# Output projection of a gated attention block: seven quarter-block products in place of eight, with float32 sums as operands

## The chip, the cores and the metric

The kernel runs on one core of one Trainium2 chip, as one launch. The metric is the device time of that launch in microseconds (us). One execution was also recorded by the hardware profiler; its times are read below. The engines are called TensorE (PE; its weight loads are PEld), VectorE (DVE), ScalarE (ACT), GpSimd (POOL) and SyncE (SP, which issues most of the transfers). Each engine works through its own list of instructions strictly in order.

## The reference

One decoder layer: a combined input projection, three attention mixers A, B and C, a gated merge, an output projection, then a SwiGLU feed-forward layer. Shapes: 512 tokens, model width 1024, hidden width 2816, all float32.

```python
h = _rms(x, norm1_g)
... = _split_last(h @ w_in, IN_SIZES)           # queries, keys, values, gates mix_g
y_a, y_b, y_c = mixer_a(...) @ w_branch_a, mixer_b(...) @ w_branch_b, mixer_c(...) @ w_branch_c
g = jax.nn.sigmoid(mix_g).reshape(bsz, seq, 3, D_MODEL)
z = g[:, :, 0] * y_a + g[:, :, 1] * y_b + g[:, :, 2] * y_c
x = x + z @ w_out                               # (512 x 1024) @ (1024 x 1024): the part that is changed
h = _rms(x, norm2_g)
gate, up = jnp.split(h @ w_ffn_in, 2, axis=-1)
x = x + (jax.nn.silu(gate) * up) @ w_ffn_out
```

## The kernel before

**Products.** Every float32 product is made of three matmuls: each operand is split into a high part (rounded by ACT) and a low part (the rest, by a DVE subtraction), and high*high, high*low and low*high are added up in PSUM (`mm3`, lines 106 to 108). The helper `split` (lines 80 to 82) makes one such pair: a cast on ACT, line 81, and a subtraction on DVE or POOL, line 82, with both inputs in SBUF. `weights` loads a slice of a weight matrix into the tile `raw` (5 buffers) and splits it into `whi` and `wlo` (6 buffers each, 128x512 elements).

**The gated merge.** For the branches in the order B, A, C and eight column blocks f of 128 each, `gate(bi, f)` makes a product of 24 matmuls into a PSUM tile `pm` (3 buffers) and takes a tanh of it on ACT into `tz`; `merge(bi, f, tz)` makes the branch product (6 matmuls for C), combines it with the gate on DVE (line 973), and adds the sum of the branches so far, which comes back from DRAM (`dz`), on POOL (line 976; on DVE for the last two blocks). For branch C the result, z transposed, stays in SBUF: `zh` is its high part (ACT, line 980) and `zl` its low part (DVE, line 981). `tz` has 3 buffers.

**The output projection** (lines 1052 to 1080). The weight is taken in four slices of 256 columns; each is loaded and split by `weights`. For each slice and each of the four token tiles t there are 8 x 3 matmuls of 256 columns, in the first slice with the last two k-blocks of all tiles held back; then DVE adds the result to the residual `x2` (line 1072), ACT takes the sum of squares, and POOL (in the last slice DVE) multiplies by the norm's gain into `xg` (line 1075). In the last slice `norm_T` is started for each token tile: a reduction, the reciprocal root on POOL, a scaled copy `hn` (half on DVE, line 176, half on ACT), 8 transposes on PE, and the split into `xh2` and `xl2`. The feed-forward layer begins with the first two token tiles as soon as these are there.

The order of the instructions on each engine is set when the program is built: a scheduler replays the program with estimated costs and lists each engine's instructions; code inside `tc.high_priority()` is taken first. Pools are stacked in SBUF; a tile in a reused place waits for the last users of that place.

Of the kernel before, what the change touches and what calls it, by code (L numbers as in the profile page):

```python
# [67 lines left out]
def block_kernel(ctx: ExitStack, tc: tile.TileContext, x, norm1_g, norm2_g, w_in, qk_norm_g, cmp_pos, cmp_w,  # L68
# [153 lines left out]
    ap_ = att.enter_context(tc.tile_pool(name="att", bufs=1, reuse_waits="tile"))  # L222
    abx = ExitStack()
# [5 lines left out]
    def bias_vectors():  # L229
# [4 lines left out]
        for c in range(0, VEC, n):  # L234
            oh = ap_.tile([NB + 1, 512], F32, name="oh", tag="p", bufs=5)
# [3 lines left out]
            vs = ap_.tile([28, 512], F32, name="vs", tag="p", bufs=5)  # L239
# [47 lines left out]
    def norm_heads(tm, c0, nh):  # L287
# [3 lines left out]
        for t in range(0, NT, 2):  # L291
            sq = ap_.tile([128, 2, 256], F32, name="sq", tag="sq", bufs=1)
# [101 lines left out]
    def scores(i):  # L394
# [34 lines left out]
    def compress_inputs():  # L429
# [10 lines left out]
        def then():  # L440
            nc.gpsimd.memset(vcp, 0.0)
            for sel in range(2):
# [18 lines left out]
                if sel == 0:  # L461
                    sq = ap_.tile([64, 64], F32, name="sqc", tag="p", bufs=5)
# [59 lines left out]
    def pt_tile(n):  # L522
        return ap_.tile([128, n, 128], F32, name="pT", tag="pT", bufs=4)
# [26 lines left out]
    def causal_probs(q, i, k, tab, topk, gate):  # L550
# [8 lines left out]
        p = ap_.tile([128, S], F32, name="p", tag="p", bufs=5)  # L559
# [41 lines left out]
    def cmp_scores(g):  # L601

        def a():
# [4 lines left out]
            sT = ap_.tile([128, S], F32, name="cmpT", tag="p", bufs=5)  # L608
# [219 lines left out]
    def c_unit(hf, i, j, ld, d):  # L828
# [6 lines left out]
        def a():  # L835
# [11 lines left out]
            p = ap_.tile([128, S], F32, name="pc_", tag="p", bufs=5)  # L847
# [111 lines left out]
    def merge(bi, f, tz):  # L959
# [48 lines left out]
    def ready(bi):  # L1008
# [21 lines left out]
    zh, zl = zs["h"], zs["l"]  # L1030
# [134 lines left out]
```

## Time and profile before

| what | value |
|---|---|
| device time, median of 3 runs | 995.63 us (993.09 to 1602.01) |
| the profiled execution, device time | 995.54 us |
| its span, from the first to the last instruction | 993.8 us |
| PE busy, share of the span | 974.3 us, 98% |
| DVE, ACT, POOL busy | 568.1, 437.5, 175.4 us |
| mean granted TensorE clock | 0.993 of full speed |

The profiled execution lies 0.09 us below the median, so times read from its trace stand for the median as they are; 1.7 us of the device time lie outside the span. The highest of the three runs stands alone and is not used. Busy shares are averages over stages with different limits; the stage of the change is 48 us long.

### The profile page before, as it was taken

The page shows a single profiled execution, that of the slowest core. Times are in us where ns is not written, and L with a number is a line of the kernel's source. Part 1 is how long each engine was busy: PE and PEld are TensorE (multiplying, and loading weights), DVE is VectorE, ACT ScalarE, POOL GpSimd, SP SyncE. Part 2 cuts the span into 40 slices and gives each one's busy share as a digit, 9 for nine tenths or more (in the row PEclk, how much of TensorE's full clock was granted, in tenths as well). Part 3 has the DMA queues.
Part 4 walks back from the last instruction along what each step waited for, and adds up shares of the span by engine and source line. Part 5 has one row for each costly group of instructions (what it writes and reads, how often), then busy time and mean ns, then how long its engine had stood idle before and what let it go on. Part 6 is the DMA issues. An engine that isn't in the chain of part 4 may idle for free.

```text
span 993.8 us, 16076 instructions
## 1 busy us (share of the span) xinstructions
PE 974.3 (98%) x5887; PEld 827.0 (83%) x5887; DVE 568.1 (57%) x1277; ACT 437.5 (44%) x956; POOL 175.4 (18%) x156
## 2 busy tenths in 40 slices
PE   6999999999999999989999999999999999999998
PEld 6889999899887578858777899988888888888886
DVE  6699999766665655665764654544344444422321
ACT  5544555755665555554543434433233233322220
POOL 4135555543100202231110312000000000000000
PEclk9999999999999899989999999999999999999999
DMA  8541344433232334346613462233333323332421
GB/s 210 122 128 44 85 119 132 123 109 122 90 104 67 85 117 138 107 141 193 180 62 97 140 210 86 85 94 108 96 85 105 107 85 91 110 97 96 138 75 42
DMA packets 119264, 109.91 MB, mean 111 GB/s; under 512 B 19931, under 2 KB 105234, under 8 KB 119186
## 3 DMA queue, kind: packets, MB, share of 16 engines
q1 hardware_dynamic: 116994, 107.85, 37.4%
q10 hardware_dynamic: 2192, 1.05, 0.4%
q8 instruction: 46, 0.75, 0.3%
q14 instruction: 32, 0.26, 0.1%
HBM read 96.66 MB, written 12.21 MB: 110 GB/s over the span
## 4 chain that ended last, share of the span: by engine, by line
PE 96%; DMA 1%; DVE 1%; ACT 1%; issue 0%; SPq 0%; DVEq 0%; ACTq 0%
PE pf L108 14%; PE pf L107 14%; PE pf L106 14%; PE pm L107 13%; PE pm L106 13%; PE pm L108 13%; PE tr L111 5%; PE ovb L541 2%; PE lg L363 2%; PE lg L364 2%; PE ova L541 1%; PE lg L843 1%; DMA raw<-in_w_in 1%; PE ovc L888 1%; PE lg L838 0%
## 5 line engine op out<-in xcount | busy, mean ns | idle before, releaser
L82 DVE TENSOR_TENSOR wlo<-raw,whi 128x512 fp32r<-128x512 f32 (+1 forms) x243 | 182.5, 756 | 147.7 <-ACT whi L81 146.6
L81 ACT CAST whi<-raw 128x512 fp32r<-128x512 f32 (+1 forms) x288 | 176.8, 619 | 173.9 <-PE pf L108 78.6
L107 PE MATMUL pm<-wlo,xh 128*128 128x256 f32 (+1 forms) x512 | 145.9, 288 | 0.3 <-DVE wlo L82 0.3
L108 PE MATMUL pm<-whi,xl 128*128 128x256 f32 (+1 forms) x512 | 145.3, 286 | 0.5 <-POOL xl L82 0.5
L106 PE MATMUL pm<-whi,xh 128*128 128x256 f32 (+1 forms) x512 | 145.7, 289 | 0.0
L107 PE MATMUL pf<-xl,whi 128*128 128x512 f32 (+1 forms) x384 | 142.6, 372 | 0.1
L106 PE MATMUL pf<-xh,whi 128*128 128x512 f32 (+1 forms) x384 | 142.5, 372 | 0.0
L108 PE MATMUL pf<-xh,wlo 128*128 128x512 f32 (+1 forms) x384 | 142.0, 371 | 0.0
L107 PEld LDWEIGHTS pm<-wlo,xh 128*128 128x128 f32 x512 | 98.5, 193 | 1.9 <-issue 0.8
L108 PEld LDWEIGHTS pm<-whi,xl 128*128 128x128 f32 x512 | 98.7, 193 | 1.4 <-POOL xl L82 0.8
L106 PEld LDWEIGHTS pm<-whi,xh 128*128 128x128 f32 x512 | 98.3, 194 | 0.4
L107 PE MATMUL pm<-xl,whi 128*128 128x512 f32 x224 | 88.8, 396 | 0.0
L108 PE MATMUL pm<-xh,wlo 128*128 128x512 f32 x224 | 88.6, 395 | 0.0
L106 PE MATMUL pm<-xh,whi 128*128 128x512 f32 x224 | 88.4, 395 | 0.0
L107 PEld LDWEIGHTS pf<-xl,whi 128*128 128x128 f32 x384 | 72.3, 188 | 12.8 <-DVE xl L82 0.3
L108 PEld LDWEIGHTS pf<-xh,wlo 128*128 128x128 f32 x384 | 72.2, 188 | 12.6
L106 PEld LDWEIGHTS pf<-xh,whi 128*128 128x128 f32 x384 | 72.2, 188 | 12.3
L82 POOL TENSOR_TENSOR wlo<-raw,whi 128x512 fp32r<-128x512 f32 x45 | 62.2, 1402 | 111.6 <-ACT whi L81 100.8
L106 PE MATMUL pf<-whi,hh 128*128 128x512 f32 x176 | 69.4, 395 | 0.0
L108 PE MATMUL pf<-whi,hl 128*128 128x512 f32 x176 | 69.4, 395 | 0.0
L107 PE MATMUL pf<-wlo,hh 128*128 128x512 f32 x176 | 69.4, 395 | 0.0
L562 ACT ACTIVATE p<-p,m 128x128 f32<-128x128 f32 (+3 forms) x96 | 53.9, 562 | 28.6 <-DVE m L547 26.4
(312 smaller groups left out, 1702.3 us busy)
## 6 DMA issues: line engine op xcount, KB each, us to landing
raw<-in_w_in SPq DMA_DIRECT2D x92, 256.0 KB, 3.0
raw<-in_w_ffn_in SPq DMA_DIRECT2D x88, 256.0 KB, 2.9
raw<-in_w_ffn_out SPq DMA_DIRECT2D x44, 256.0 KB, 2.8
raw<-in_w_in SPq DMA_DIRECT2D x52, 128.0 KB, 2.4
x<-in_x SPq DMA_DIRECT2D x8, 512.0 KB, 5.9
tab<-dvec SPq DMA_DIRECT2D x16, 256.0 KB, 3.3
dz<-tz SPq DMA_DIRECT2D x16, 256.0 KB, 2.4
tz<-dz SPq DMA_DIRECT2D x16, 256.0 KB, 3.3
```

Source lines behind the costliest of these rows:

```text
L81: nc.scalar.copy(dst_hi, src)
L82: (eng or nc.vector).tensor_tensor(out=dst_lo, in0=src, in1=dst_hi.bitcast(F32), op=ALU.subtract)
L106: nc.tensor.matmul(ps, ah, bh, start=(j == 0), stop=False)
L107: nc.tensor.matmul(ps, ah, bl, start=False, stop=False)
L108: nc.tensor.matmul(ps, al, bh, start=False, stop=(j == n - 1))
L111: nc.tensor.transpose(dst, src, ident[0:src.shape[0], 0:src.shape[0]])
L363: nc.tensor.matmul(lg, qs, k[:, 0, 0:w], start=True, stop=False)
L364: nc.tensor.matmul(lg, qs, k[:, 1, 0:w], start=False, stop=stop)
L541: mm = nc.tensor.matmul(ov[64 * j:64 * j + 64, 128 * b:S], v(b), pts[j][:, 4 * b:3 * b + NT, :], start=first and b == 0, stop=last and b = ...
L562: nc.scalar.activation(p[:, 0:w], p[:, 0:w], AF.Exp, bias=m[:, 0:1], scale=-1.0, accum_out=m[:, 1:2])
L843: nc.tensor.matmul(lg[32 * r:32 * r + 32, c:c + n], ld["q", g][hp, 128 * i + 32 * r:128 * i + 32 * r + 32], ld["k", g][hp, 128 * r:128 * r ...
L888: nc.tensor.matmul(ov[h, 128 * b_:128 * q1], ld["v", 0][:, b_, h], d["pt", jj][:, 2 * b_:b_ + q1, :], start=b_ == 0, stop=False)
```

## The change

The projection z @ w_out is cut into quarter blocks: z by token halves and by even and odd blocks f (A11: second half of the tokens, even blocks; A12: the same, odd; A22: first half, odd), w_out into B11, B12, B21, B22 (k-halves by columns 0 to 511 and 512 to 1023). With sums of quarter blocks as further operands (S1 to S4 of z, T1 to T4 of w_out) seven products of 256 x 512 x 512 take the place of eight. Each product is 2 token tiles x 4 k-blocks x 3 matmuls, now of 512 columns.

What is moved and added: the weight is loaded whole by `wo_load`, in four transfers of 1 MB during branch C, into a pool of its own; that place is freed by closing a part of the attention pool early (`att2`, which is the former `att` without two tags). T3 and T2 are made on POOL at once, T1 and T4 on POOL later (`wo_operands`). `z_parts` replaces the split of each z block: per pair of blocks four sums on DVE of 128x256 and the splits of A11, of the odd block, of S2 and S4, and of S1 and S3. The seven weight operands are each split by ACT and DVE (28 splits for 16). Partial results are collected in `zu` and added to `x2` on POOL (`pool_add`), or added straight from PSUM on DVE (`add_half`).

```diff
@@ pools and places (the same edit for the tags p, sq and pT) @@
+    att2 = ExitStack()
+    a2 = att2.enter_context(tc.tile_pool(name="att2", bufs=1, reuse_waits="tile"))
...
-        p = ap_.tile([128, S], F32, name="p", tag="p", bufs=5)
+        p = a2.tile([128, S], F32, name="p", tag="p", bufs=5)
...
@@ merge, branch C @@
-            nc.scalar.mul(zs["h"][:, f, :], th, 0.5)
-            nc.vector.scalar_tensor_tensor(out=zs["l"][:, f, :], in0=th, scalar=0.5, in1=zs["h"][:, f, :].bitcast(F32),
-                                           op0=ALU.mult, op1=ALU.subtract)
+            z_parts(f // 2, f % 2, th)
+
+    T1, T2 = slice(S // 2, S), slice(0, S // 2)
+    WO_AT = (0, 2, 3, 5)
+
+    def wo_load(m):
+        raw = zs["raw"][m]
+        nc.sync.dma_start(raw, w_out[m * 256:(m + 1) * 256, :].rearrange("(k p) (n c) -> p k n c", p=128, n=2))
+        b11, b12, b22, t2 = raw[:, 0, 0, :], raw[:, 0, 1, :], raw[:, 1, 1, :], zs["t2"][m]
+        nc.gpsimd.tensor_tensor(out=b12, in0=b22, in1=b12, op=ALU.subtract)
+        nc.gpsimd.tensor_tensor(out=t2, in0=b12, in1=b11, op=ALU.add)
+
+    def z_parts(m, odd, th):
+        if not odd:
+            zs["even"] = th
+            split(zs["a11"][:, 0, m, :], zs["a11"][:, 1, m, :], th[:, T1])
+            return
+        e = zs["even"]
+        sums = []
+        for _ in range(2):
+            sums.append(zs["p"].tile([128, 2, S // 2], F32, name="zsum", tag="zsum", bufs=2))
+        (s2, s4), (s1, s3) = ([t_[:, j, :] for j in range(2)] for t_ in sums)
+        nc.vector.tensor_tensor(out=s1, in0=e[:, T2], in1=th[:, T2], op=ALU.add)
+        nc.vector.tensor_tensor(out=s2, in0=s1, in1=e[:, T1], op=ALU.subtract)
+        nc.vector.tensor_tensor(out=s4, in0=th[:, T1], in1=s2, op=ALU.subtract)
+        split(zs["s24"][:, 0, m], zs["s24"][:, 1, m], sums[0])
+        split(zs["o"][:, 0, m, :], zs["o"][:, 1, m, :], th)
+        nc.vector.tensor_tensor(out=s3, in0=e[:, T1], in1=e[:, T2], op=ALU.subtract)
+        split(zs["s13"][:, 0, m], zs["s13"][:, 1, m], sums[1])
...
+                if due[0][0] == 2 and due[0][1] in WO_AT:
+                    wo_load(WO_AT.index(due[0][1]))
                 merge(*due.pop(0))
...
@@ output projection @@
-    for c in range(0, D, 256):
-        wk = weights(w_out, [(c, 256)], list(range(KC)))
...
-            mm3(pss[t][:, 0:256], [((zh[:, k, ts], zl[:, k, ts]), wk[k]) for k in range(k0, k1)], k0, KC)
...
-            nc.vector.tensor_tensor(out=xs, in0=xs, in1=pss[t][:, 0:256], op=ALU.add)
...
+                if name == "t1":
+                    nc.gpsimd.tensor_tensor(out=b11, in0=b22, in1=t2, op=ALU.subtract)
+                elif name == "t4":
+                    nc.gpsimd.tensor_tensor(out=t2, in0=b21, in1=t2, op=ALU.subtract)
+                hi = wp.tile([128, 512], F32R, name="whi", tag="whi")
+                lo = wp.tile([128, 512], F32R, name="wlo", tag="wlo")
+                split(hi, lo, src)
...
+    def add_half(t, cs, ps):
+        nc.vector.scalar_tensor_tensor(out=x2[t][:, cs], in0=ps, scalar=0.5, in1=x2[t][:, cs], op0=ALU.mult, op1=ALU.add)
...
+    def pool_add(t, cs, u):
+        nc.gpsimd.tensor_tensor(out=x2[t][:, cs], in0=x2[t][:, cs], in1=u, op=ALU.add)
+
+    for a, b in (("a11", "b11"), ("s2", "t2"), ("a12", "b21"), ("s3", "t3"), ("s1", "t1"), ("a22", "t4"), ("s4", "b22")):
+        ws = wo_operands(b)
+        for r in range(2):
+            ps, t1, t2 = m2_tile(), NT // 2 + r, r
+            if b == "b22" and r == 1:
+                product(a, ws, ps, r, range(2))
+                next(norms[1], None)
+                product(a, ws, ps, r, range(2, HK))
+            else:
+                product(a, ws, ps, r)
+            if b == "b11":
+                us[r] = zs["p"].tile([128, 512], F32, name="zu", tag="zsum", bufs=2)
+                nc.scalar.mul(us[r], ps, 0.5)
+                pool_add(t1, C1, us[r])
+            elif b in ("t2", "t3"):
+                nc.vector.scalar_tensor_tensor(out=us[r], in0=ps, scalar=0.5, in1=us[r], op0=ALU.mult, op1=ALU.add)
+                for t, cs in ((t1, C2),) if b == "t2" else ((t2, C2), (t2, C1)):
+                    pool_add(t, cs, us[r])
+            elif b == "b21":
+                add_half(t1, C1, ps)
+                done(t1, C1, nc.gpsimd)
+            elif b == "t1":
+                add_half(t2, C2, ps)
+                add_half(t1, C2, ps)
+                done(t2, C2, nc.gpsimd)
+            elif b == "t4":
+                add_half(t2, C1, ps)
+                done(t2, C1, nc.vector)
+                norm2(t2)
+            else:
+                add_half(t1, C2, ps)
+                done(t1, C2, nc.vector)
+                norm2(t1)
+                if r == 0:
+                    next(norms[0], None)
```

Up to the merges of branch C the lists of all engines are the same as before, instruction by instruction. On POOL, from the first z block of branch C on, the list before held only the six sums with `dz` and then the multiplications by the gain:

```order
L976 TENSOR_TENSOR tz_6543<-tz_6543 128x512
L976 TENSOR_TENSOR tz_6587<-tz_6587 128x512
L976 TENSOR_TENSOR tz_6662<-tz_6662 128x512
L976 TENSOR_TENSOR tz_6701<-tz_6701 128x512
L976 TENSOR_TENSOR tz_6770<-tz_6770 128x512
L976 TENSOR_TENSOR tz_6809<-tz_6809 128x512
L1075 TENSOR_TENSOR xg0_6975<-x2_0_6960,gb2_6973 128x256
```

In the changed kernel eight sums of the weight (`wraw`, `wt2`) stand between the sums of the z blocks (`tz`); the first rows are:

```order
L993 TENSOR_TENSOR wraw0_6601<-wraw0_6601 128x512
L994 TENSOR_TENSOR wt2_0_6605<-wraw0_6601 128x512
L978 TENSOR_TENSOR tz_6546<-tz_6546 128x512
L993 TENSOR_TENSOR wraw1_6602<-wraw1_6602 128x512
L978 TENSOR_TENSOR tz_6590<-tz_6590 128x512
L994 TENSOR_TENSOR wt2_1_6606<-wraw1_6602 128x512
L978 TENSOR_TENSOR tz_6679<-tz_6679 128x512
L993 TENSOR_TENSOR wraw2_6603<-wraw2_6603 128x512
L993 TENSOR_TENSOR wraw3_6604<-wraw3_6604 128x512
L994 TENSOR_TENSOR wt2_2_6607<-wraw2_6603 128x512
L994 TENSOR_TENSOR wt2_3_6608<-wraw3_6604 128x512
L978 TENSOR_TENSOR tz_6728<-tz_6728 128x512
```

The first weight pair now stands ahead of the first z block, and weight sums ahead of most later ones; eight more (lines 1102 and 1104) and eight additions to `x2` (line 1139) follow behind.

On DVE, around the last two merges of branch C, the list before had two gate products, two sums and the two low parts of z, and then went on to the weight splits of the projection:

```order
L973 SCALAR_TENSOR_TENSOR tz_6878<-tz_6878,pm_6926 128x512
L976 TENSOR_TENSOR tz_6878<-tz_6878 128x512
L973 SCALAR_TENSOR_TENSOR tz_6917<-tz_6917,pm_6938 128x512
L82 TENSOR_TENSOR wlo_7132<-raw_7129,whi_7131 128x512
L976 TENSOR_TENSOR tz_6917<-tz_6917 128x512
L981 SCALAR_TENSOR_TENSOR zl_6594<-tz_6878,zh_6593 128x512
L981 SCALAR_TENSOR_TENSOR zl_6594<-tz_6917,zh_6593 128x512
L82 TENSOR_TENSOR wlo_7138<-raw_7135,whi_7137 128x512
```

In the changed kernel the same two merges (line 975) bring three low parts of z sums (`za11`, `zo`, `zs13`, and `zs24` of the pair before) and four sums `zsum`:

```order
L975 SCALAR_TENSOR_TENSOR tz_6921<-tz_6921,pm_6982 128x512
L82 TENSOR_TENSOR zs24_6599<-zsum_6936,zs24_6599 128x512
L978 TENSOR_TENSOR tz_6921<-tz_6921 128x512
L975 SCALAR_TENSOR_TENSOR tz_6973<-tz_6973,pm_6994 128x512
L82 TENSOR_TENSOR wlo_7102<-wt2_1_6606,whi_7101 128x512
L1011 TENSOR_TENSOR zsum_7004<-tz_6921 128x256
L82 TENSOR_TENSOR za11_6597<-tz_6921,za11_6597 128x256
L978 TENSOR_TENSOR tz_6973<-tz_6973 128x512
L1006 TENSOR_TENSOR zsum_7004<-tz_6921,tz_6973 128x256
L1007 TENSOR_TENSOR zsum_7003<-zsum_7004,tz_6921 128x256
L82 TENSOR_TENSOR zo_6598<-tz_6973,zo_6598 128x512
L1008 TENSOR_TENSOR zsum_7003<-tz_6973,zsum_7003 128x256
```

The weight splits `wlo` of the second product, which PE needs next, now stand between and behind these rows.

## Rows read from the trace of the kernel before

**Rows 1.** The page: span, engine totals, PE in 40 slices, chain by engine, ACT's casts.

```profile
span 993.8 us, 16076 instructions
...
PE 974.3 (98%) x5887; PEld 827.0 (83%) x5887; DVE 568.1 (57%) x1277; ACT 437.5 (44%) x956; POOL 175.4 (18%) x156
...
PE   6999999999999999989999999999999999999998
...
PE 96%; DMA 1%; DVE 1%; ACT 1%; issue 0%; SPq 0%; DVEq 0%; ACTq 0%
...
L81 ACT CAST whi<-raw 128x512 fp32r<-128x512 f32 (+1 forms) x288 | 176.8, 619 | 173.9 <-PE pf L108 78.6
```

**Rows 2.** Busy time by stage: branch C's merges, projection, feed-forward; columns as headed.

```profile
core 0: us, PE busy (x) PEld busy (x) DVE busy (x) ACT busy (x) POOL busy (x), PEclk, DMA share, GB/s
540.00:576.40 36.40, 36.40 (x162) 30.10 (x161) 23.73 (x30) 16.21 (x27) 9.20 (x6) 1.00 0.46 138
576.40:624.40 48.00, 48.00 (x402) 47.93 (x401) 23.89 (x46) 21.05 (x54) 12.68 (x18) 1.00 0.41 132
645.00:840.00 195.00, 195.00 (x884) 162.39 (x884) 84.39 (x126) 64.94 (x108) 0.00 (x0) 1.00 0.35 98
```

**Rows 3.** Timeline of PE: starts of 512-column matmuls, then 256-column ones.

```profile
548.08 0.39 PE L106 MATMUL pm<-xh,whi 128*128 128x512 f32 x1
...
551.25 0.39 PE L108 MATMUL pm<-xh,wlo 128*128 128x512 f32 x1
...
614.81 0.28 PE L106 MATMUL pf<-whi,zh 128*128 128x256 f32 x1
...
619.61 0.28 PE L107 MATMUL pf<-wlo,zh 128*128 128x256 f32 x1
```

**Rows 4.** Durations by tile (ns min/median/max): DVE's subtraction, POOL's sum.

```profile
L82 DVE TENSOR_TENSOR wlo<-raw,whi x122: 684/693/697, 649.3 to 974.0; 128x512 fp32r<-128x512 f32 x122
...
L976 POOL TENSOR_TENSOR tz<-tz x7: 1288/1622/1745, 520.2 to 569.5; 128x512 f32<-128x512 f32 x7
```

**Rows 5.** Timeline, POOL and DVE, 546 to 551 and 625 to 627.

```profile
546.60 2.99 POOL L976 TENSOR_TENSOR tz<-tz 128x512 f32<-128x512 f32 x2 [24.79 <-DVE tz L973]
...
545.77 1.28 DVE L973 SCALAR_TENSOR_TENSOR tz<-tz,pm 128x512 f32<-128x512 f32 x2 [0.47 <-PE pm L108]
546.98 3.16 DVE L82 TENSOR_TENSOR wlo<-raw,whi 128x512 fp32r<-128x512 f32 x2
...
625.65 0.41 DVE L1072 TENSOR_TENSOR x<-x,pf 128x256 f32<-128x256 f32 x1
625.98 1.29 DVE L82 TENSOR_TENSOR wlo<-raw,whi 128x512 fp32r<-128x512 f32 x2
```

**Rows 6.** Timeline of DVE and PE: the last norm steps, first feed-forward matmuls.

```profile
616.95 0.49 DVE L176 TENSOR_SCALAR hn<-xg,rst 128x512 f32<-128x512 f32 x1 [0.96 <-POOL rst L151]
...
619.73 1.03 PE L111 MATMUL pf<-ident,hn 128*128 128x128 f32 x8
...
624.35 0.28 PE L108 MATMUL pf<-whi,zl 128*128 128x256 f32 x1
624.47 0.28 PE L106 MATMUL pf<-xh,whi 128*128 128x256 f32 x1
```

**Rows 7.** PE's longest wait inside the kernel, and the granted clock around it.

```profile
435.54 0.87 PE L111 MATMUL tr<-ident,p 128*128 128x128 f32 x3 [3.49 <-DVE p L564]
...
426.00:433.50 7.50, 5.98 (x35) 4.14 (x29) 6.16 (x12) 3.98 (x12) 4.74 (x5) 1.00 0.33 92
433.50:440.50 7.00, 4.23 (x18) 3.25 (x18) 4.70 (x11) 3.54 (x8) 1.68 (x2) 0.51 0.30 89
```

**Rows 8.** Transfers: last attention matmuls on PE, and what a busy stretch moved.

```profile
537.42 1.96 PE L893 MATMUL ovc<-pt,c_v 128*64 128x128 f32 x29
...
577.00:584.00 7.00, 7.00 (x61) 7.00 (x60) 3.09 (x5) 1.40 (x3) 0.00 (x0) 1.00 0.72 232
```

More of the change, by code (lines that the diff above doesn't have):

```diff
@@ L522, in pt_tile @@
     def pt_tile(n):
-        return ap_.tile([128, n, 128], F32, name="pT", tag="pT", bufs=4)
+        return a2.tile([128, n, 128], F32, name="pT", tag="pT", bufs=4)
     def transposed(pt, p, i):
@@ L846, in a @@
             w = w0 + 2 * n
-            p = ap_.tile([128, S], F32, name="pc_", tag="p", bufs=5)
+            p = a2.tile([128, S], F32, name="pc_", tag="p", bufs=5)
             m = ty.tile([128, 4], F32, name="mcc", tag="m")
@@ L1015, in ready @@
         czx.close()
+        att2.close()
         zp = zx.enter_context(tc.tile_pool(name="zs", bufs=1, side="right", reuse_waits="tile"))
-        zs["h"] = zp.tile([128, KC, S], F32R, name="zh")
-        zs["l"] = zp.tile([128, KC, S], F32R, name="zl")
+        zs["p"] = zp
+        zs["a11"] = zp.tile([128, 2, KC // 2, S // 2], F32R, name="za11")
+        zs["o"] = zp.tile([128, 2, KC // 2, S], F32R, name="zo")
+        zs["s24"] = zp.tile([128, 2, KC // 2, 2, S // 2], F32R, name="zs24")
+        zs["s13"] = zp.tile([128, 2, KC // 2, 2, S // 2], F32R, name="zs13")
+        zs["raw"] = [zp.tile([128, 2, 2, 512], F32, name=f"wraw{m}") for m in range(KC // 2)]
+        zs["t2"] = [zp.tile([128, 512], F32, name=f"wt2_{m}") for m in range(KC // 2)]
     due = []
@@ new lines, in block_kernel, with wo_operands @@
+    norms = {}
+    HK = KC // 2
+    def wo_operands(name):
+        res = []
+        with tc.high_priority():
+            for m in range(HK):
+                raw, t2 = zs["raw"][m], zs["t2"][m]
+                b11, t3, b21, b22 = (raw[:, k, n, :] for k in range(2) for n in range(2))
+                src = {"b11": b11, "b21": b21, "b22": b22, "t1": b11, "t2": t2, "t3": t3, "t4": t2}[name]
+                if name == "t1":
[5 more added lines that the diff above has]
+                split(hi, lo, src)
+                res.append((hi, lo))
+        return res
@@ new lines, in block_kernel, with product @@
+    z_rows = {"a11": lambda p, m: zs["a11"][:, p, m, :], "a12": lambda p, m: zs["o"][:, p, m, T1],
+              "a22": lambda p, m: zs["o"][:, p, m, T2], "s2": lambda p, m: zs["s24"][:, p, m, 0, :],
+              "s4": lambda p, m: zs["s24"][:, p, m, 1, :], "s1": lambda p, m: zs["s13"][:, p, m, 0, :],
+              "s3": lambda p, m: zs["s13"][:, p, m, 1, :]}
+    us = [None, None]
+    C1, C2 = slice(0, 512), slice(512, D)
+    def product(a, ws, ps, r, ms=range(HK)):
+        rs = slice(128 * r, 128 * r + 128)
+        for m in ms:
+            (ah, al), (bh, bl) = (z_rows[a](p, m)[:, rs] for p in range(2)), ws[m]
+            nc.tensor.matmul(ps, ah, bh, start=m == 0, stop=False)
+            nc.tensor.matmul(ps, ah, bl, start=False, stop=False)
+            nc.tensor.matmul(ps, al, bh, start=False, stop=m == HK - 1)
@@ new lines, in add_half, with done, norm2 @@
+    def add_half(t, cs, ps):
+        nc.vector.scalar_tensor_tensor(out=x2[t][:, cs], in0=ps, scalar=0.5, in1=x2[t][:, cs], op0=ALU.mult, op1=ALU.add)
+    def done(t, cs, eng):
+        norm_sums(ss2[t], x2[t], np_, cs.start, cs.stop, 1)
+        eng.tensor_tensor(out=xg[t][:, cs], in0=x2[t][:, cs], in1=gb2[:, cs], op=ALU.mult)
+    def norm2(t):
+        norms[t] = norm_T(xg[t], t, ss2[t], 2, None, xh2, xl2, lambda: m2_tile().rearrange("p (k c) -> p k c", c=128), np_,
+                          (nc.vector, nc.vector))
+        next(norms[t])
```

40 lines of the change are left out of this document (8 added, 32 removed).

## The prediction

> **What bounds the kernel now.** I read the page first: PE is busy for 974.3 of 993.8 us and makes up 96% of the chain that ended last [rows 1]. The reader is to see that only PE's path counts, as long as nobody makes PE wait. Then the stages [rows 2]: in the merges of branch C and in the projection PE works without a gap (36.4 of 36.4 and 48.0 of 48.0 us), DVE fills 23.7 us of the first and 23.9 of the second, POOL 9.2 and 12.7; in the feed-forward layer PE has no gap either. So the change is worth what it takes from PE between 546 and 625 us, unless DVE or POOL, which get much more to do there, fall behind. The third view is therefore the timeline of DVE and POOL where both work at once [rows 5].
>
> **The matmuls.** From 548.08 to 551.25 PE starts 14 matmuls of 512 columns after the first, 0.2264 us each; from 614.81 to 619.61 it starts 40 of 256 columns, 0.120 us each [rows 3]. Before: 4 slices x 4 token tiles x 8 blocks x 3 = 384 x 0.120 = 46.1 us. After: 7 products x 2 x 4 x 3 = 168 x 0.2264 = 38.0 us. PE saves **8.1 us**; the transposes stay.
>
> **What DVE and POOL cost each other.** Alone, a DVE subtraction of 128x512 with both inputs in SBUF takes 0.69 us (0.60 from start to start: two take 1.29), a POOL sum 1.29 [rows 4, 5]. At 546.60 POOL starts two sums, and DVE behind it two subtractions; DVE ends at 546.98 + 3.16 = 550.14, so two of each took 3.54 us, 1.77 for a pair. That is the sum of the two (1.29 + 0.48), not the longer one: they take turns. The two DVE operations just before, with one input in PSUM, took 1.28 us together, as ever, though POOL had started within them [rows 5]: these don't take turns. The Trainium skill says the same in "SBUF — State Buffer", section "Who interferes with whom": a DVE instruction with two SBUF inputs and a GpSimd instruction that reads SBUF exclude each other for their whole length. By that rule the new POOL sums are no free help to DVE, and this trace agrees (1.77 us a pair).
>
> So I add up, as one queue, all that must pass that turnstile from POOL's first z sum at 546.60 to the norm's `hn` of the first token tiles, which starts at 616.95 before [rows 6].
> - POOL: 6 z sums, 6 weight sums of `wo_load` (the first two come ahead of 546.60), 8 sums for T1 and T4, 8 additions to `x2`, 4 multiplications by the gain: 32 x 1.29 = 41.3 us.
> - DVE, 128x512, both inputs in SBUF: 7 splits left of the gates and branch C, 28 of w_out, 2 of the feed-forward weight, 12 low parts of z, 2 sums with `dz`, 3 gains: 54, at 0.48 to 0.60 (rows as above). I take 0.55, between the two: 29.7 us (25.9 to 32.4).
> - DVE, 128x256: 4 low parts of A11 and 16 sums, at 0.33 (the start-to-start time of the 256-column row at 625.65 [rows 5]): 6.6 us.
>
> Together 77.6 us (73.8 to 80.3). DVE also runs 19 operations with an input in PSUM, 0.60 each, 11.4 us. They cost nothing where POOL uses the turnstile meanwhile. From the lists: for 9 of them POOL's next operation needs their result, during 2 POOL waits for a later split, and for the last 3 POOL has nothing left; 14 x 0.60 = 8.4 us are exposed (0 to 11.4). `hn` then starts at 546.6 + 77.6 + 8.4 = 632.6 (620.4 to 638.3), 15.6 us later than before.
>
> **From there to the feed-forward layer.** Before, its first matmul starts at 624.47, 7.5 us after `hn`, because PE still has two token tiles to multiply. After, PE has only the second half of the seventh product left: `hn` 0.5, 8 transposes 1.0, 12 matmuls 2.7, 8 transposes 1.0, a cast 0.6, together 5.8 us [rows 1, 3, 6]. So it starts at 638.4, **13.9 us later** (1.7 to 19.6). The rest is PE's alone, as before. This is not added to the 8.1 us: they are saved on an engine that now waits.
>
> **Who waits.** In the merges: POOL's sum of a z block stands behind weight sums, DVE's sums behind it, and `tz` has three buffers, so a tanh waits for the sums of the block three before, `pm` is freed late and PE's next merge waits. In the projection: PE's tenth matmul needs A11 of block 6, which is behind two merges' work on DVE; later PE waits for single `wlo` tiles, and before the last half product for `hn`. All this is inside the sum.
>
> **The clock.** After PE's one long wait (3.49 us) the granted clock is 0.51 of full speed, 1.2 in place of 2.4 GHz, from 433.5 to 440.5 us [rows 7]. Such a stretch costs up to 3.5 us where PE is the bound. The waits above are as long, three of them. Two fall where DVE and POOL set the pace and PE has time to spare; the last stands ahead of the feed-forward layer, where it counts. I take +2.3 us (0 to 7, two stretches).
>
> **Hidden.** ACT gets 12 more weight casts, about 6 more z casts and 2 copies, 20 x 0.62 = 12 us, and has 84.4 - 37.3 = 47 us free [rows 1, 2]. SP: the four 1 MB transfers can't start before the last attention matmuls leave their place, about 539.4; at the 232 GB/s of a busy stretch [rows 8] the first lands near 544 and the fourth near 557.5, about when POOL's queue comes to it. The gate weights queued behind them on SP come later, too; I take 0 (0 to +3).
>
> **Sum.** 995.5 (profiled, 0.1 below the median) + 13.9 + 2.3 = **1011.7 us**; its own range goes from 995.5 + 1.7 = 997 to 995.5 + 19.6 + 7 = 1022. A difference of 2% (19.9 us) is about what a measurement of this kernel can tell from no change; this one is 1.6%.
>
> **Rivals.**
> - *PE's saving stands* (not slower): DVE and POOL keep ahead, as they would if their turns overlapped: DVE's and POOL's own times are then no bound, and PE's 8.1 us come off: 987.4. For it: DVE was half idle in both stages. Against: the pair of 1.77 us; and even the smallest sum, 73.8 us with nothing exposed, ends `hn` after 616.95.
> - *The clock decides* (slower by over 2%): each long wait of PE starts a stretch at half clock, in which PE becomes the bound, too, and the DVE operations that wait for PSUM results come later. It decides from the third stretch that counts: 995.5 + 13.9 + 3 x 3.5 = 1019.9. For it: the wait of 3.49 us before such a stretch [rows 7] is no longer than these; against: PE would have spare time in two of the three.
> - *The weight comes late*: SP's queue or the transfers hold POOL's first weight sum, and with it every z block, by up to 3 us: 1014.7. The list puts that sum ahead of the first z block, so there is no way around it.
>
> **How the numbers follow.** Forecast 0.63; saving stands 0.09; clock 0.21; weight late 0.07. The predicted time is 1011.7. For 8 in 10 I leave out most of the saving (below) and the clock's upper end: 995 to 1025. Over 2% faster (below 975.7) is reached by no case; I leave 0.01. Slower by over 2% (above 1015.5): the clock rival and a part of the forecast's upper end, 0.28. Within 2%: 0.71.
>
> **What would show it.** In the changed profile: DVE's `wlo` and z operations between 546 and 632 at well over 1 us in the mean where 0.69 is their time alone, DVE and POOL almost without common idle time, PE busy for about two thirds of the projection; PE waiting in its first product for the cast of `za11`, and for `hn` before its last half product; the first feed-forward matmul near 638; matmuls of 512 columns still 0.226 us apart where nothing waits; a granted clock below 1.00 after the waits. Wrong it would be if the weight and z operations of DVE stay near 0.7 us while POOL is busy, or if PE's list runs through without waits: then the saving stands. If the merges of branch C end at 576.7 as before, the waits in them were not there.

## The result, and the profile of the changed kernel

The changed kernel takes 1007.69 us (median; 1005.00 to 1010.67) against 994.98 us for the kernel before: a ratio of 1.0135, 95% interval 1.0096 to 1.0174. That median of the kernel before counts a run of 1602.01 us that stands alone; its other three runs have a median of 994.33, and the ratio is against them. The prediction was 1011.7 us with a range of 995 to 1025. So seven products in place of eight made the kernel about 13 us slower. The profiled execution took 1007.67 us, its span is 1005.9, 12.1 more than before.

The page of the changed kernel, first the span, the engines' totals, TensorE (PE) in 40 slices, and the chain that ended last by engine:

```profile
span 1005.9 us, 15679 instructions
...
PE 971.7 (97%) x5671; PEld 813.6 (81%) x5671; DVE 609.0 (61%) x1311; ACT 445.5 (44%) x962; POOL 209.8 (21%) x172
...
PE   6999999999999999989999978999999999999998
...
PE 87%; DVE 5%; DMA 3%; issue 2%; SPq 1%; ACT 1%; POOL 1%; DVEq 0%; POOLq 0%; ACTq 0%
```

PE is busy 2.6 us less than before [rows 1], but the span grew, and the chain runs only for 87% over PE where it was 96%. The slices show where: the two that cover 578 to 629 us, in the projection, have 7 and 8 where they had 9.

Busy time by stage, in the first two windows of [rows 2] and then in four pieces of the projection:

```profile
core 0: us, PE busy (x) PEld busy (x) DVE busy (x) ACT busy (x) POOL busy (x), PEclk, DMA share, GB/s
540.00:576.40 36.40, 34.87 (x156) 28.41 (x154) 31.42 (x38) 15.42 (x28) 21.09 (x15) 1.00 0.51 161
576.40:624.40 48.00, 42.34 (x171) 33.14 (x169) 47.93 (x56) 23.36 (x45) 32.34 (x20) 0.93 0.16 60
580.00:592.20 12.20, 6.60 (x20) 4.93 (x19) 12.13 (x17) 3.69 (x7) 6.18 (x4) 0.72 0.63 236
592.20:624.00 31.80, 31.77 (x137) 25.26 (x135) 31.80 (x36) 17.43 (x34) 23.73 (x14) 1.00 0.00 1
624.00:636.00 12.00, 7.05 (x31) 5.60 (x29) 9.72 (x20) 8.06 (x17) 2.32 (x6) 0.72 0.24 66
```

In the projection the engines have changed places. VectorE (DVE) is busy for 47.93 of 48.00 us where it was 23.89, and PE, which had no gap, has 5.7 us of them. The granted clock is 1.00 except in the two short windows where PE waited.

What PE waited for between 540 and 640 us (total, times, longest):

```profile
PE pf L1122 <- ACT za L81: 5.6, 1, 5.6
PE pf L111 <- DVE hn L176: 4.6, 1, 4.6
PE pm L106 <- ACT tz L958: 1.5, 1, 1.5
PE pf L107 <- DVE nss L170: 0.6, 1, 0.6
PE pf L106 <- ACT xh L81: 0.3, 1, 0.3
```

These are 12.6 us, and the three long ones are at places that the prediction named: the merges, the tenth matmul of the first product, and the transposes of `hn` before the last half product. The timeline of PE around the wait for `hn` and the first feed-forward matmul (start, length, engine, line, operation):

```profile
623.99 0.39 PE L1124 MATMUL pf<-whi,zs 128*128 128x512 f32 x1
629.00 1.97 PE L111 MATMUL pf<-ident,hn 128*128 128x128 f32 x8 [4.63 <-DVE hn L176]
630.62 0.77 PE L1122 MATMUL pf<-whi,zs 128*128 128x512 f32 x1
631.20 0.63 PE L1123 MATMUL pf<-wlo,zs 128*128 128x512 f32 x1
631.62 0.63 PE L1124 MATMUL pf<-whi,zs 128*128 128x512 f32 x1
632.05 0.63 PE L1122 MATMUL pf<-whi,zs 128*128 128x512 f32 x1
632.48 0.63 PE L1123 MATMUL pf<-wlo,zs 128*128 128x512 f32 x1
632.90 0.47 PE L1124 MATMUL pf<-whi,zs 128*128 128x512 f32 x1
633.21 0.39 PE L1122 MATMUL pf<-whi,zs 128*128 128x512 f32 x1
633.45 0.39 PE L1123 MATMUL pf<-wlo,zs 128*128 128x512 f32 x1
...
634.38 0.40 PE L1124 MATMUL pf<-whi,zs 128*128 128x512 f32 x1
634.62 1.04 PE L111 MATMUL pf<-ident,hn 128*128 128x128 f32 x8
635.97 0.39 PE L106 MATMUL pf<-xh,whi 128*128 128x256 f32 x1 [0.32 <-ACT xh L81]
```

Three things stand in these rows. The first feed-forward matmul starts at 635.97; before it was 624.47 [rows 6]. After the wait the matmuls of 512 columns come 0.43 us apart (631.20 to 632.48: 3 in 1.28 us), the pace of the lower clock level. And at the full clock they come 0.234 us apart (633.21 to 634.38: 5 in 1.17 us), not the 0.2264 us that the gate's matmuls of the same width have [rows 3].

The timelines of VectorE and then GpSimd (POOL) in the middle of the projection:

```profile
594.03 1.78 DVE L82 TENSOR_TENSOR wlo<-wt,whi 128x512 fp32r<-128x512 f32 x1
595.74 6.40 DVE L82 TENSOR_TENSOR wlo<-wraw,whi 128x512 fp32r<-128x512 f32 x5
602.06 0.68 DVE L1156 SCALAR_TENSOR_TENSOR zu<-pf,zu 128x512 f32<-128x512 f32 x1
```

```profile
593.66 1.61 POOL L1104 TENSOR_TENSOR wt<-wraw,wt 128x512 f32<-128x512 f32 x1 [4.09 <-DVE wlo L82]
595.96 1.62 POOL L1104 TENSOR_TENSOR wt<-wraw,wt 128x512 f32<-128x512 f32 x1 [0.69 <-DVE wlo L82]
597.54 3.44 POOL L1139 TENSOR_TENSOR x<-x,zu 128x512 f32<-128x512 f32 x2
```

Five subtractions took 6.40 us beside three of POOL's operations. Alone, five take 4 x 0.60 + 0.69 = 3.1 us [rows 4, 5], so POOL's three cost VectorE 3.3 us. The single subtraction before them shows the turn itself: it starts at 594.03, 0.37 us into a sum of POOL's that ends at 595.27, and ends at 595.81, 0.54 us behind that sum.

**Where the 12.1 us came from.** The last attention matmuls end at 538.46 + 1.96 = 540.42, 1.04 us later than before [rows 8]: that difference is ahead of the change. In the merges 1.8 us are lost, 1.5 of them the wait for `tz`. The projection, from its first matmul (576.65 before, 579.53 now) to the first of the feed-forward layer, takes 56.44 us in place of 47.82, that is +8.6: its matmuls take 168 x 0.2333 = 39.2 us in place of 46.1 (-6.9), three waits add 5.60 + 4.63 + 0.32 = 10.55, and half clock adds 4.1 (from 587.38, 11 matmuls in 4.81 us where 2.57 would do; from 629.00, 8 transposes and 6 matmuls in 4.21 us, which take 2.34 in a run below that fills this wait); 0.9 is left over. Another 0.6 is the wait for `nss` behind it.

### The profile page after: what moved, and what is told of

Read it like the earlier page. It is cut to its first block, busy times and chain, and to the rows that moved or that the text cites. A ratio compares the mean times of both kernels' runs of the same rounds, so it can differ in the third digit from the quotient of the medians.

```text
span 1005.9 us, 15679 instructions
## 1 busy us (share of the span) xinstructions
PE 971.7 (97%) x5671; PEld 813.6 (81%) x5671; DVE 609.0 (61%) x1311; ACT 445.5 (44%) x962; POOL 209.8 (21%) x172
## 4 chain that ended last, share of the span: by engine, by line
PE 87%; DVE 5%; DMA 3%; issue 2%; SPq 1%; ACT 1%; POOL 1%; DVEq 0%; POOLq 0%; ACTq 0%
PE pf L107 12%; PE pf L108 12%; PE pf L106 12%; PE pm L107 11%; PE pm L106 11%; PE pm L108 11%; PE tr L111 5%; PE ovb L543 2%; PE lg L365 2%; PE lg L366 2%; DVE wlo L82 2%; PE pf L1122 1%; PE ova L543 1%; PE pf L1123 1%; PE pf L1124 1%
## 5 line engine op out<-in xcount | busy, mean ns | idle before, releaser
L82 DVE TENSOR_TENSOR wlo<-raw,whi 128x512 fp32r<-128x512 f32 (+1 forms) x227 | 170.9, 757 | 138.6 <-ACT whi L81 138.1
L81 ACT CAST whi<-raw 128x512 fp32r<-128x512 f32 (+1 forms) x272 | 166.9, 619 | 164.0 <-PE pf L108 76.1
```

The lines of the kernel that those rows point to most:

```text
L81: nc.scalar.copy(dst_hi, src)
L82: (eng or nc.vector).tensor_tensor(out=dst_lo, in0=src, in1=dst_hi.bitcast(F32), op=ALU.subtract)
```

## The experiments

My theory was the turnstile of the prediction: an operation of VectorE with two inputs in SBUF and one of POOL take turns, and the queue that they form sets `hn`. The rivals: VectorE's own work is too much, whoever makes the sums; the clock; something in the seven products themselves (their order, their pace, the transfers). Eleven kernels were run. The times are medians beside runs of the kernel before on the same chip; ratios are against the kernel before. On those chips the kernel before had medians of 994.99 to 996.05 us. The last attention matmul, ahead of the merges of branch C, ends between 537.5 and 540.8 us in the profiled executions, so the table counts `hn` from there.

| kernel | median us | ratio, 95% interval | `hn` behind the last attention matmul, us |
|---|---|---|---|
| before | 994.98 | 1 | 77.6 |
| changed | 1007.69 | 1.0135 (1.0096 to 1.0174) | 88.0 |
| e1, weight sums on VectorE | 1000.2 | 1.0047 (1.0031 to 1.0062) | 83.2 |
| e2, all those sums on VectorE | 1000.67 | 1.0049 (1.0032 to 1.0067) | 82.2 |
| e3, no operand sums | 994.43 | 0.9987 (0.9971 to 1.0004) | 76.6 |
| e5, before with 512 columns | 997.13 | 1.0024 (1.0002 to 1.0046) | 79.7 |
| e7, e2 in another order | 997.74 | 1.0028 (1.0014 to 1.0043) | 80.5 |
| e8, e1 in another order | 997.75 | 1.0020 (1.0005 to 1.0034) | 77.4 |
| e9, e3 in another order | 990.28 | 0.9938 (0.9921 to 0.9955) | 71.3 |
| e10, before with more POOL sums | 997.53 | 1.0015 (1.0000 to 1.0030) | 79.9 |
| e11, changed with waits filled | 1004.62 | 1.0096 (1.0082 to 1.0110) | 88.9 |
| e12, e7 with the wait filled | 997.78 | 1.0022 (1.0007 to 1.0036) | 79.9 |
| e13, changed in another order | 1004.09 | 1.0088 (1.0075 to 1.0101) | 83.4 |

### e1 and e2: the sums on VectorE

e1 moves the 16 weight sums:

```
-        nc.gpsimd.tensor_tensor(out=b12, in0=b22, in1=b12, op=ALU.subtract)
-        nc.gpsimd.tensor_tensor(out=t2, in0=b12, in1=b11, op=ALU.add)
+        nc.vector.tensor_tensor(out=b12, in0=b22, in1=b12, op=ALU.subtract)
+        nc.vector.tensor_tensor(out=t2, in0=b12, in1=b11, op=ALU.add)
...
-                    nc.gpsimd.tensor_tensor(out=b11, in0=b22, in1=t2, op=ALU.subtract)
+                    nc.vector.tensor_tensor(out=b11, in0=b22, in1=t2, op=ALU.subtract)
...
-                    nc.gpsimd.tensor_tensor(out=t2, in0=b21, in1=t2, op=ALU.subtract)
+                    nc.vector.tensor_tensor(out=t2, in0=b21, in1=t2, op=ALU.subtract)
```

> The changed kernel with its 16 weight sums issued on VectorE in place of GpSimd (14 of them behind the first z sum); nothing else moves. Theory of the turns (an operation of VectorE with two SBUF inputs and one of GpSimd exclude each other): each sum that leaves GpSimd takes 1.29 us out of the queue and brings back 0.55 us on VectorE, so hn starts 14 x 0.74 = 10.4 us sooner than its 628.5, near 618, and the time falls from 1007.7 to about 997 (995 to 1000). Rival of volume (VectorE is simply the fuller engine, GpSimd's sums ran beside it for nothing): 14 x 0.55 to 0.69 = 7.7 to 9.7 us more in VectorE's queue, hn near 637, the time 1015 to 1017. Rival of the clock (the half-clock stretches set the loss): they stay, and so does the time, 1005 to 1011.

e2 moves the eight additions of `pool_add` and four gains as well:

```
-        nc.gpsimd.tensor_tensor(out=x2[t][:, cs], in0=x2[t][:, cs], in1=u, op=ALU.add)
+        nc.vector.tensor_tensor(out=x2[t][:, cs], in0=x2[t][:, cs], in1=u, op=ALU.add)
...
-                done(t1, C1, nc.gpsimd)
+                done(t1, C1, nc.vector)
...
-                done(t2, C2, nc.gpsimd)
+                done(t2, C2, nc.vector)
```

> As the run with the weight sums moved, and the eight additions of the shared partial sum and the four gain products moved to VectorE as well (26 operations behind the first z sum in all; six z sums and the small rstd operations stay on GpSimd). Turns: 26 x 0.74 = 19.2 us out of the queue, hn near 609.3; the time would be 988.5, down to where TensorE's own work ends it (994.98 - 8.1 = 986.9). Volume: 26 x 0.55 to 0.69 = 14.3 to 17.9 us more, 1022 to 1026. Clock: unchanged at 1005 to 1011. If VectorE alone becomes the bound once the turns are gone, the time stops falling between the run with the weight sums moved and this one.

e1 took 1000.2 us and e2 1000.67. In the groups of VectorE from 540 to 632 us (count, busy us, mean ns, idle before), the subtractions of w_out in the changed kernel:

```profile
L82 DVE TENSOR_TENSOR wlo<-wraw,whi 128x512 fp32r<-128x512 f32 x20 | 21.4, 1111 | 0.0
...
L82 DVE TENSOR_TENSOR wlo<-wt,whi 128x512 fp32r<-128x512 f32 x8 | 8.6, 1080 | 0.0
```

in e1:

```profile
L82 DVE TENSOR_TENSOR wlo<-wraw,whi 128x512 fp32r<-128x512 f32 x20 | 19.9, 1026 | 0.0
...
L82 DVE TENSOR_TENSOR wlo<-wt,whi 128x512 fp32r<-128x512 f32 x8 | 8.0, 1017 | 0.0
```

and in e2:

```profile
L82 DVE TENSOR_TENSOR wlo<-wraw,whi 128x512 fp32r<-128x512 f32 x20 | 13.2, 684 | 0.2 <-ACT whi L81 0.2
...
L82 DVE TENSOR_TENSOR wlo<-wt,whi 128x512 fp32r<-128x512 f32 x8 | 5.4, 682 | 0.0
```

The same 28 subtractions, on the same data, take 684 and 682 ns where POOL has nothing beside them, and 1111 and 1080 where it has: that VectorE is held is shown, and that giving VectorE more to do makes the kernel faster speaks against the rival of volume in its plain form. But the size was wrong. 26 operations moved behind the first z sum brought `hn` forward by 5.8 us (88.0 to 82.2), 0.22 each and not 0.74, and the second dozen brought only 0.9 of them. In e2 VectorE is busy for 76.2 of the 80.6 us from 540 to `hn`, only some 4 of them held, by POOL's six z sums: its own work is then the bound, as the last sentence of the expectation allowed.

### e3 and e9: without the sums

e3 leaves the sums out and multiplies what is there:

```
-        nc.vector.tensor_tensor(out=s1, in0=e[:, T2], in1=th[:, T2], op=ALU.add)
-        nc.vector.tensor_tensor(out=s2, in0=s1, in1=e[:, T1], op=ALU.subtract)
-        nc.vector.tensor_tensor(out=s4, in0=th[:, T1], in1=s2, op=ALU.subtract)
-        split(zs["s24"][:, 0, m], zs["s24"][:, 1, m], sums[0])
...
-              "a22": lambda p, m: zs["o"][:, p, m, T2], "s2": lambda p, m: zs["s24"][:, p, m, 0, :],
+              "a22": lambda p, m: zs["o"][:, p, m, T2], "s2": lambda p, m: zs["a11"][:, p, m, :],
```

and so on for s1, s3 and s4 and the four kinds of weight sums. What comes out is not the layer's result; the matmuls and transfers are the same.

> The changed kernel without the sums that make the operands: it leaves out the 16 weight sums and the 16 sums of z with the splits of s1 to s4, and multiplies parts of z and blocks of the weights that are there already, in the same seven products (same matmuls, same transfers, same weight casts). If the loss is all in making the operands, TensorE's saving stands alone: the queue loses 14 x 1.29 + 16 x 0.33 + 8 x 0.55 = 27.7 us, hn would be free at 601 and TensorE ends it, 994.98 - 8.1 = 986.9 (985 to 991). If part of the loss is the order of the seven products, the transfers or the pools, it stays above 995.

It took 994.43 us: not slower than before any more, but not 986.9 either. So making the sums, with the splits of s1 to s4, is what costs the 13 us. Most of the saving was still missing, and VectorE had 16.5 us idle ahead of `hn` (58.4 of 74.9 us from 540 busy). PE's long waits between 540 and 640 us were these:

```profile
PE pf L111 <- DVE hn L176: 3.4, 1, 3.4
PE pf L107 <- DVE nss L170: 1.0, 1, 1.0
```

The suspect was the order of the products: token tiles 0 and 1 are completed by the sixth, and only one product is left to cover their norm. So e9 moves the third product, which serves tiles 2 and 3 alone, to the sixth place:

```
-    for a, b in (("a11", "b11"), ("s2", "t2"), ("a12", "b21"), ("s3", "t3"), ("s1", "t1"), ("a22", "t4"), ("s4", "b22")):
+    for a, b in (("a11", "b11"), ("s2", "t2"), ("s3", "t3"), ("s1", "t1"), ("a22", "t4"), ("a12", "b21"), ("s4", "b22")):
```

> As the run without the operands' sums (the same parts left out: the 16 weight sums, the 16 sums of z and the splits of s1 to s4), with the third product moved to the sixth place. Tail: its waits of 3.4 us for hn and 1.0 us for nss go and nothing else is late, since VectorE has 16.5 us idle ahead of hn; all of TensorE's 8.1 us appear: 986.9 to 990, against 994.4 without the move. If the missing 4 us were something else (the seven products' own pace, the transfers), it stays at 993 to 996.

990.28 us, ratio 0.9938. The waits for `hn` and `nss` are gone; PE waited for the first `xh` and `xl` only:

```profile
PE pf L106 <- ACT xh L81: 1.2, 1, 1.2
PE pf L107 <- DVE xl L82: 0.9, 1, 0.9
```

So of the missing part some 4 us were the order. The rest is the pace: at 0.2333 us a matmul the seven products save 6.9 us, not 8.1, and 2.1 us of waits are left, so that 4.8 us should come off; the ratio says 6.2 (4.5 to 7.9).

### e7, e8 and e13: the order alone

The same line moved, in e2 (e7), in e1 (e8) and in the changed kernel (e13).

> As the run with all sums on VectorE, with one more edit: the third product (rows a12 with block b21) becomes the sixth, so that two products and not one stand behind the pair that completes token tiles 0 and 1. Theory of the tail (a part of the saving is lost because hn of tile 0 is asked for one product after its last addition): what the old third product puts ahead of hn in VectorE's queue, 4 subtractions, 2 additions and 2 gains of 0.68 us = 5.5 us, stands behind hn now, hn starts near 615 in place of 620.6, TensorE's wait of 5.9 us for it goes, and the time falls from 1000.7 to 994 to 996. Rival (VectorE's whole sum is the bound, 76.2 of the 80.6 us to hn): the wait only changes its name, to the subtractions of the last two products, and the time stays at 999 to 1001.

> As the run with the weight sums on VectorE, with the third product moved to the sixth place. Tail: its wait of 2.3 us for hn goes, from 1000.2 to about 998. VectorE's whole sum: no change, 999 to 1001; the half-clock stretch that followed the waits may stay in either.

> The changed kernel with the third product moved to the sixth place and nothing else. By what the move was worth with the sums on VectorE (2.5 and 2.9 us): 1007.7 - 2.7 = 1005 (1003.5 to 1006.5). If GpSimd's own queue sets hn (its 12 operations behind the weight sums keep their order and their number): 1007 to 1009.

It was worth 2.9, 2.5 and 3.6 us in the medians: more than nothing in each. For e7 that is about half of what the theory of the tail said: 997.74 us lies between its 994 to 996 and the rival's 999 to 1001. In e7 `hn` came only 1.7 us sooner (80.5 for 82.2), not 5.5, because the subtractions for the last two products are issued at high priority and still stand ahead of it: PE's wait for `hn` fell from 5.9 to 4.0 us and did not vanish. The rival was right that VectorE's whole sum remains the bound there. In e8 and e13 the wait for `hn` did vanish, and waits of 4.1 and 2.5 us for ScalarE's (ACT's) `xh`, one step further down the same path, took its place.

### e5: PE's part alone, in the kernel before

e5 keeps the eight products and makes the matmuls of the projection 512 columns wide:

```
-    for c in range(0, D, 256):
-        wk = weights(w_out, [(c, 256)], list(range(KC)))
+    for c in range(0, D, 512):
+        wk = weights(w_out, [(c, 512)], list(range(KC)), 1)
...
-            if last:
-                proj(t, 0, 4)
-                if t > 1:
-                    next(norms[t - 2], None)
-            proj(t, KC - 2 if first else 4 if last else 0, KC)
+            proj(t, 0, k1)
+        for t in range(NT):
+            if last and t > 1:
+                next(norms[t - 2], None)
+            proj(t, k1, KC)
```

with `k1` six blocks in the first pass and four in the last, all token tiles up to `k1` first.

> The kernel before with its eight products kept and only their width changed: two passes of 512 columns in place of four of 256, 192 matmuls of 0.2264 us for 384 of 0.120 us. If TensorE's saving counts where it is made, 46.1 - 43.5 = 2.6 us come off: 992.4 (991 to 994). If the projection's end waits for VectorE already, nothing or a loss: each of the last four blocks is twice as wide, and what VectorE does behind it, an addition, a square, a gain and the norm, starts later by half a block: 995 to 998.

997.13 us, ratio 1.0024: the second expectation. Two things ate the 2.6 us. The pace is 0.233 us here, too (13 matmuls in 3.03 us from 599.74 to 602.77), so only 46.1 - 44.8 = 1.3 were to be had; and PE waits 2.5 us for the first `xh`, behind which the clock halves (matmuls of 256 columns 0.21 us apart from 626.3 to 628.9 us).

### e10: the turnstile without the queue

e10 gives POOL twenty more sums in the kernel before, whose results nobody uses:

```
+    def more_sum(a, b):
+        o = zs["p"].tile([128, S], F32, name="more", tag="more", bufs=2)
+        nc.gpsimd.tensor_tensor(out=o, in0=a.bitcast(F32), in1=b.bitcast(F32), op=ALU.add)
...
         else:
+            more_sum(xh[:, 0, :], xl[:, 0, :])
...
+            if not last:
+                more_sum(zh[:, 0, :], zl[:, 0, :])
```

> The kernel before with 20 sums of 128x512 more on GpSimd, whose results nobody uses: one in each of the eight merges of branch C, one behind each addition of the projection's first three column blocks. Turns with a free queue: VectorE's subtractions beside them grow to about 1.7 us (the mean of wlo above its 815 ns), 20 x 0.8 to 1.1 = 16 to 22 us more held time on VectorE, which has 34.7 us idle ahead of hn, so the time stays within 0.5%: 994 to 999. Rival (a GpSimd sum that holds VectorE costs the path wherever it is, about 0.8 us each): 1008 to 1012. Third: nothing is held, mean of wlo stays 815 ns, 995.

997.53 us, ratio 1.0015 (1.0000 to 1.0030). Seven of the twenty ran ahead of 540 us and the other thirteen between 540 and 576 us, earlier than I had meant, since their inputs were there. VectorE and POOL in 540 to 632 us:

```profile
L82 DVE TENSOR_TENSOR wlo<-raw,whi 128x512 fp32r<-128x512 f32 x32 | 32.5, 1048 | 6.1 <-ACT whi L81 6.1
L986 DVE SCALAR_TENSOR_TENSOR zl<-tz,zh 128x512 fp32r<-128x512 f32 x8 | 9.4, 1185 | 5.4 <-ACT zh L985 5.3
...
L961 POOL TENSOR_TENSOR more<-zh,zl 128x512 f32<-128x512 f32 x12 | 19.6, 1667 | 0.0
...
L961 POOL TENSOR_TENSOR more<-xh,xl 128x512 f32<-128x512 f32 x1 | 1.7, 1744 | 0.0
```

The same two groups of VectorE in the kernel before:

```profile
L82 DVE TENSOR_TENSOR wlo<-raw,whi 128x512 fp32r<-128x512 f32 x32 | 25.5, 815 | 11.4 <-ACT whi L81 10.8 <-DMA raw<-in_w_out 0.4
L981 DVE SCALAR_TENSOR_TENSOR zl<-tz,zh 128x512 fp32r<-128x512 f32 x8 | 6.5, 825 | 2.7 <-ACT zh L980 2.6
```

The mean of the subtractions rose to 1048 ns, not to the 1.7 us that was expected. The thirteen sums cost VectorE 32 x 0.233 + 8 x 0.360 = 10.3 us, 0.8 us each, and the kernel next to nothing (1.5 us by the ratio, 0 to 3.0; PE waited 1.5 us): VectorE had that time. The price is paid on VectorE; whether it reaches the end depends on how full VectorE is.

### e11 and e12: the waits filled, for the clock

e11 puts matmuls of no use into the two long waits of the changed kernel:

```
+    def fill(a, ws, m, n):
+        d = m2_tile()
+        for _ in range(n):
+            nc.tensor.matmul(d, z_rows[a](0, m)[:, 0:128], ws[m][0], start=True, stop=True)
...
+            if a == "a11" and r == 0 and m == 3:
+                fill(a, ws, 0, 22)
...
                 if r == 0:
+                    fill(a, ws, 3, 18)
                     next(norms[0], None)
```

e12 is e7 with only the second place filled, with 16 matmuls.

> The changed kernel with matmuls of no use in TensorE's two long waits: 22 of 128x512 ahead of the tenth matmul of the first product (22 x 0.233 = 5.1 us, the wait there is 5.6) and 18 ahead of the first transposes of hn (4.2 us, the wait is 4.63). They end before what TensorE waits for is there, so they add nothing to the path. Theory of the clock as a part of the loss: the granted clock no longer halves at 585 and 626, 11 matmuls go at 0.233 in place of 0.427 us (2.1 us) and the first transposes with 5 matmuls behind them take 2 us less: 1007.7 - 4 = 1003.5 (1002.5 to 1005). Rival (the queue of VectorE sets the end anyway, a faster TensorE waits longer): 1007 to 1009. If the filling itself delays something, over 1009.

> The run with all sums on VectorE and the third product sixth, with 16 matmuls of no use (3.7 us) ahead of the first transposes of hn, where TensorE waits 4.0 us and the clock halves from 617.5 to 623.5. Clock: 2 to 2.5 us come off 997.7, to 995.2 to 995.7, no slower than the kernel before. Rival (VectorE's queue sets the end): 997 to 999.

e11 took 1004.62 us, 3.1 less than the changed kernel in the medians. That is in the expected 1002.5 to 1005, but the two intervals overlap, so the gain is read from the trace, and only one of the two places did what it was meant to: the second. PE in e11, the end of the filling, the transposes and the matmuls behind them:

```profile
626.45 2.50 PE L1121 MATMUL pf<-whi,zs 128*128 128x512 f32 x10
629.16 1.09 PE L111 MATMUL pf<-ident,hn 128*128 128x128 f32 x8 [0.21 <-DVE hn L176]
630.01 0.48 PE L1129 MATMUL pf<-whi,zs 128*128 128x512 f32 x1
...
631.50 0.40 PE L1129 MATMUL pf<-whi,zs 128*128 128x512 f32 x1
...
634.49 0.39 PE L106 MATMUL pf<-xh,whi 128*128 128x256 f32 x1 [0.55 <-ACT xh L81]
```

The clock stays at full speed there, and from `hn` (628.6, as in the changed kernel) to the first feed-forward matmul it is 5.9 us in place of 7.5. At the first place it failed: the filling writes a PSUM tile of its own, and that place came free only with VectorE's last read of branch C's products (the operation that writes `tz`), so it waited 2.4 us itself, the granted clock was 0.66 from 583 to 588, and the first product came no sooner. In e12 the filling took the wait of 4.0 us for the first `hn` away, and the first feed-forward matmul came 1.9 us sooner behind the last attention matmul than in e7 (86.3 for 88.2). But the half-clock stretch came at 628.0 to 631.7 instead (granted clock 0.54), behind waits of 1.1 us for `xh` and 0.5 for a later `hn`; from the first feed-forward matmul to the end e12 takes 2.1 us more than e7 (371.4 for 369.3), and the time stayed at 997.78. So the clock is a real part of the loss at the second wait of the changed kernel, 1.6 to 1.9 us in the traces; it isn't the part that decides.

No version that computes the layer with seven products beat the kernel before: the best (e7, e8, e12) are 0.2 to 0.3% slower.

## Why the prediction was right, and where its terms were off

**The mechanism** (PE's saving lies on an engine that waits; VectorE and POOL hold each other; `hn` comes late) was right, and so were the three places of the waits and the sign. The rule of the Trainium skill ("SBUF — State Buffer", section "Who interferes with whom") says that such operations exclude each other for their whole length; 684 against 1111 ns for the same subtractions agrees, and so does the subtraction at 594.03, which ended 0.54 us behind POOL's sum. The counterpart of that rule for operations with one input in SBUF agrees as well: the additions to `x2` that read PSUM took 677 ns in the changed kernel and 683 in e2. Of the signs that it named, VectorE's long operations and the lack of common idle time came (1111 ns; from the first z sum to `hn` VectorE and POOL were both idle for 0.2 us in all). Others did not: PE was busy for 88% of the window from 576.4 to 624.4 us and not for two thirds, PE's matmuls did not wait for single `wlo` tiles between 540 and 640 us, and the matmuls of 512 columns came 0.2333 us apart, not 0.226.

**The queue's sum** gave `hn` at 632.6; it was 628.5, of which 1.04 had come from ahead of the change: +10.5 us and not +15.6. Two errors in it partly cancelled. POOL's 32 operations were put in at 1.29 us each, 41.3; what they cost VectorE is the excess of its operations' means in 547.6 to 628.5 us over 684 ns (512 columns) and 415 ns (256), which they take in e2: 27.4 us, 0.86 each (0.8 in e10). The rest of POOL's time ran beside the operations that read PSUM, or went first. In turn VectorE's own work was too small: from start to start 54 operations at 0.60 us, 20 at 0.34 and 20 with PSUM inputs at 0.60, none of them free, are 51.2 us, not 29.7 + 6.6 + 8.4 = 44.7. 51.2 + 27.4 + 1.4 idle = 80.0, and 80.9 passed from the first z sum (547.6) to `hn`. The single queue was the wrong picture of a right effect: the queue is VectorE's, POOL's operations lengthen it by 0.86 us each, and an operation moved over saves only 0.86 - 0.60 = 0.26 (0.22 measured). The expectations of e1 and e2 failed by this step. That the predicted time came within 4 us is luck in part: POOL's term was 13.9 us too large, VectorE's 6.5 too small.

**PE's saving** of 8.1 us was mis-sized: 6.9, since the 512-column matmuls of the projection come at 0.2333 us. **From `hn` to the feed-forward layer** it was 7.5 us, not 5.8, because of the half clock there, which the forecast had counted as a term of its own: the first feed-forward matmul came 11.5 us later, half clock included, where 13.9 + 2.3 = 16.2 was forecast.

**The clock** was put at +2.3; the two stretches cost 4.1 us of PE's time, 2.2 of them while VectorE set the pace. The rival in which it decides fell by this size: it asked for three stretches that count, and e11, which kept the second place at full clock though not the first, stayed 0.96% slower. **The weight** wasn't late. But the reason given was wrong, too: SP's queue issued the first two transfers at 531.0 and 531.5 us and the other two at 540.5 and 540.9, not all from 539.4, and POOL's first weight sum ran at 539.4, ahead of the merges. SP and POOL of the changed kernel:

```profile
531.00 10.34 SPq L991 DMA_DIRECT2D wraw<-in_w_out  x4
...
539.36 1.27 POOL L993 TENSOR_TENSOR wraw<-wraw 128x512 f32<-128x512 f32 x1 [16.52 <-DMA wraw<-in_w_out]
```

**The rival that PE's saving stands** fell in the changed kernel, since VectorE did not keep ahead. But VectorE and POOL were not all that stood in its way: with the sums left out most of the saving was still missing (e3), and it took the order of the products as well to bring most of it out (e9). The prediction had named the wait for `hn` before the last half product, but inside VectorE's and POOL's queue, not as a loss that stays when the queue is short. A term for that loss is what it lacked.

**Left open.** Why the 512-column matmuls of the projection are 0.007 us slower than the gate's was not tried. The parts above leave 0.9 us of the projection's 8.6 without a name. In e12 the trace shows where the 1.9 us went, but not why the clock fell there behind waits of 1.1 and 0.5 us and stayed at full speed in e11 behind one of 0.55.

## What to carry to other kernels

Count what a change adds to every engine in the stage, and not only what it takes from the one that bounds it: here 6.9 us less on TensorE cost VectorE 41 us more of busy time ahead of `hn` (83.4 for 42.3), where it had 35 free. Some 22 of the 41 are time for which POOL held it (28 us for 6, by the excess used above). Price a helper engine's operation by what it takes from the engine that it holds, and look for idle time there first: thirteen more sums took 10 us of VectorE's time and cost the kernel some 1.5 us where VectorE had it, and moving sums from POOL to VectorE saved a quarter of a microsecond each where it hadn't. And when products are reordered or made larger, put the ones that the next stage doesn't ask for last: that one line was worth 2.5 to 4.2 us in the medians of all four versions.

## What the runs showed of the hardware that was not expected

- 512-column matmuls of the projection start 0.2333 us apart at the full granted clock, in the changed kernel, in e5 and in e9; those of the gates 0.2264. At the lower level they start 0.427 us apart.
- A GpSimd sum of 128x512, 1.29 us alone, costs VectorE 0.8 to 0.86 us on average, not its length.
- Filling a wait of TensorE with matmuls of no use kept the granted clock at full speed at one place (e11) and only moved the half-clock stretch 10 us on at another (e12), behind waits of 1.1 and 0.5 us.
